# The first modulation of a transformer block: from column sums to rows turned into columns

## The chip, the cores and the metric

The kernel runs as one program on one core of a Trainium2 chip. The metric is the device time of one execution in microseconds; the times of before are the median of three runs. The trace comes from one more, profiled execution.

## The reference

Two transformer blocks run one after the other over 512 tokens of width 1024; this change lies at the very beginning of the first. There the vector c (1024 numbers) is turned into a shift and a scale for every channel, and the normed input is modulated with them before the first projection:

```
c_act = silu(c)
mod   = c_act @ w_ada + b_ada               # w_ada: 1024 x 6144
sh1, sc1, gt1, sh2, sc2, gt2 = split(mod, 6)
h     = rmsnorm(x, g_mix) * (1 + sc1) + sh1
proj  = h @ w_in                            # 1024 x 2560
```

Only sh1 (columns 0 to 1023 of w_ada) and sc1 (columns 1024 to 2047) are wanted at once; they are 8 MB of weights. The other four parts are computed later, beside other work. After `proj` follow an attention with differences of two softmaxes, a pooling, a gated convolution, a gated feed-forward layer, and a second block with three attentions and a large mixture of experts.

## The kernel before

Everything is kept transposed: channels on the 128 partitions, eight chunks of 128 channels (`xT[:, k, :]`, k from 0 to 7), 512 tokens along the free dimension. A product of full precision is made from split operands: each weight block and each chunk of h is cut into a high part (a copy to fp32r on ACT, `wh` in L87, `hh` in L556) and a low part (the difference on VectorE, `wl` in L90, `hl` in L559), and `product` issues three matrix products of 512 columns, high x high (L431), high x low (L432), low x high (L433).

The program's order is written out by hand: each engine executes its instructions in the order in which the code issues them, and waits there for what they need. A `Stream` loads weight blocks of 512 KB on SP's queue into four buffers (`wr`), and splits each when the code asks for it (`stream.until`, `stream.get`).

The opening goes like this. SP's queue loads two modulation blocks, x in eight pieces, more modulation blocks, the first three blocks of `w_in`, and the rest of the modulation blocks; ACT's queue loads c broadcast to all partitions (`cb`) and small vectors, POOL's queue two constants. The modulation is computed in two ways. A block `ada[j]` holds 128 output channels on the partitions and 1024 inputs along the free dimension; VectorE multiplies it by silu(c), held on all partitions (`silc`), and sums along the row into one column of `mod` (`mod_chunk`, L331). This is done for the eight chunks of the shift and, as `ADAP` is 4, for the first four of the scale. The last four chunks of the scale are sums on TensorE (`scale_sums`, L516): a 128 x 128 piece of weights is the stationary side, one column of silu(c) (`silk`) moves, and eight of those add up into one column of `ps_sc`.

Beside this, the squares of x are added up chunk by chunk (L411, L414 on ACT, L415 on VectorE), TensorE sums them over the channels (`token_sums`, L391), VectorE takes the reciprocal root in small steps (`rsqrt`, L369 to L377), and TensorE and ACT spread it over the partitions (L384, L543).

The first three blocks of `w_in` are then multiplied as one group (`gemm2`): for each chunk k, `h_ready(k)` issues the making of `hh[k]`, of the next chunk's scaled input (`full`, L551) and of `hl[k]`, and the modulation of chunk k + 2; then the nine products of chunk k follow. What leaves the group is split again and sent through a bounce buffer in memory (`restack`) to be laid out for the attention.

Of the kernel before, what the change touches and what calls it, by code (L numbers as in the profile page):

```python
# [33 lines left out]
ORDER_IN2 = [0, 4, 8, 1, 5, 9, 2, 6, 10, 3, 7, 11, 16, 12, 17, 13, 32, 22, 23, 14, 27, 24, 25, 15, 41,  # L34
              26, 35, 18, 19, 34, 36, 28, 44, 20, 37, 21, 45, 29]
ADA_FROM = 4
ADAP = 4
NADA = 3
MEMA = 4
NU = 2  # L40
# [198 lines left out]
def tile_kernel(ctx, tc, a, out):  # L239
# [77 lines left out]
    for i in range(7):  # L317
        tag = "e" if i < P["es"] else "wt"
        ada0.append(wk.tile([128, D], F32, name="ada0", tag=tag, bufs=P["es"] if tag == "e" else 7 - P["es"]))
    cb = wraw.tile([128, D], F32, name="wr")  # L320
    nc.scalar.dma_start(cb, bass.AP(tensor=a["c"].tensor, offset=0, ap=[[0, 128], [1, D]]))
    b_ada = load("b_ada", [128, 48], nc.scalar)
    mod = cst.tile([128, 48], F32, name="mod")
    silc = cst.tile([128, D], F32, name="silc")
    vec = {"g_mix": load("g_mix", [128, 8], nc.scalar)}
    silk = load("c_cols", [128, 8], nc.scalar)
    identf = load("identf", [128, 128], nc.scalar)

    def mod_chunk(key, w):
        j = key[1]  # L330
# [4 lines left out]

    stream.made = made

    def load_ada(*js):
        for j in js:
            nc.sync.dma_start(ada0[j], a["ada"][j] if j < 8 + ADAP else a["ada_sc"][j - 8 - ADAP])  # L340
    load_ada(0, 8)
    for k in range(KD):
        nc.sync.dma_start(xT[:, k, :], a["xT"][:, k, :])
    load_ada(12, 1, 9, 13)
    stream.RAW = 3
    stream.load()
    ada0.append(wraw.tile([128, D], F32, name="wr"))
    load_ada(14, 15, 2, 10, 3, 11, 4, 5, 6, 7)
    nc.scalar.activation(silk, silk, AF.Silu)
    nc.scalar.activation(silc, cb, AF.Silu)  # L350
    ones = cst.tile([128, 1], F32, name="ones")
    nc.vector.memset(ones, 1.0)

# [157 lines left out]
    nc.vector.tensor_scalar(b_sc, b_ada[:, 8:16], 1.0, None, op0=OP.add)  # L511
    ps_sc = pst.tile([128, 512], F32, name="pt")

    def scale_sums(k):
        for i in range(KD):
            nc.tensor.matmul(ps_sc[:, k:k + 1], ada0[8 + k][:, 128 * i:128 * i + 128], silk[:, i:i + 1],  # L516
                             start=i == 0, stop=i == KD - 1)

    def modulation(k):
        mod_chunk(("ada", k), ada0[k])  # L520
        if k < ADAP:
            mod_chunk(("ada", 8 + k), ada0[8 + k])
            nc.vector.scalar_tensor_tensor(gs[:, k:k + 1], mod[:, 8 + k:9 + k], 1.0, vec["g_mix"][:, k:k + 1],
                                           op0=OP.add, op1=OP.mult)
            return
        nc.vector.scalar_tensor_tensor(gs[:, k:k + 1], ps_sc[:, k:k + 1], b_sc[:, k:k + 1], vec["g_mix"][:, k:k + 1],
                                       op0=OP.add, op1=OP.mult)

    modulation(0)
    acc = SumSq(S)  # L530
    for k in range(KD):
        tag, n = (("hsq", 2), ("hqs", 2), ("hi", 2), ("lo", 2))[k // 2]
        acc.add(xT[:, k, :], tmp=hn.tile([128, 512], F32, name="sq0", tag=tag, bufs=n))
    stream.ahead = 0
    stream.until(("w_in", ORDER_IN[0]))
    scale_sums(4)
    modulation(1)
    r0 = rsqrt(acc.sums(), [128, 4], 1.0 / D, EPS)
    scale_sums(5)
    stream.until(("w_in", ORDER_IN[2]))  # L540
    Rs = hn.tile([128, S], F32, name="rs0", tag="hqs")
    R = spread(r0, 4)
    nc.scalar.activation(Rs, R, AF.Copy)  # L543
    for k in range(6, KD):
        scale_sums(k)

    hf = {}

# [4 lines left out]

    def h_ready(k):

        nc.scalar.activation(hh[:, k, :], hf[k], AF.Identity, bias=mod[:, k:k + 1])  # L556
        if k + 1 < KD:
            scaled(k + 1)
        nc.vector.scalar_tensor_tensor(hl[:, k, :], hf.pop(k), mod[:, k:k + 1], hh[:, k, :].bitcast(F32),  # L559
                                       op0=OP.add, op1=OP.subtract)  # L560
        if k + 2 < KD:
            modulation(k + 2)


    def head_norm(src, n, g, nh, then, sq=None, qs=None, scaled=False, floor=None):
# [1517 lines left out]
def layout(i):  # L2083
    i = {k: np.asarray(v) for k, v in i.items()}
    r = consts()
    tr = lambda x: np.ascontiguousarray(x[0].T.reshape(KD, 128, -1).transpose(1, 0, 2))
    r["xT"] = tr(i["x"])
    r["mem"] = i["mem_2"].reshape(2, 128, D)
    r["c"] = i["c"].reshape(D)
    r["ada"] = np.ascontiguousarray(i["w_ada"][0].T).reshape(48, 128, D)  # L2090
    r["ada_sc"] = blocks(i["w_ada"][0][:, 128 * (8 + ADAP):2048], 8)
    r["c_cols"] = cols(i["c"])
    r["b_ada"] = cols(i["b_ada"])
    for n, m in (("g_mix", "g_mix"), ("g_ffn", "g_ffn"), ("g_final", "g_final"), ("norm1_g", "norm1_g_2"),
                 ("norm2_g", "norm2_g_2"), ("mem_norm_g", "mem_norm_g_2"), ("g_subln", "g_subln"),
                 ("pool_scale", "pool_scale")):
        r[n] = cols(i[m])
    r["conv_w"] = np.ascontiguousarray(i["conv_w"][0].reshape(3, 2, 128).transpose(2, 1, 0))
    for n in ("lambda_q1", "lambda_k1", "lambda_q2", "lambda_k2"):
        r[n] = i[n].reshape(32)  # L2100
    r["w_in"] = blocks(i["w_in"][0], 8)
    r["w_mem_kv"] = blocks(i["w_mem_kv_2"][0], 8)
    r["w_out"] = blocks(i["w_out"][0], 8)
    r["w_gate_up"] = blocks(i["w_gate_up"][0], 8)
    wd = i["w_down"][0]
    dn = np.zeros((24, 128, 1024), np.float32)
    for g, (f0, f1) in enumerate(FGROUPS):
        dn[8 * g:8 * g + 8, :, :128 * (f1 - f0)] = blocks(wd[128 * f0:128 * f1], f1 - f0)
    r["w_down"] = dn
    wp = np.zeros((128, 2, 128), np.float32)  # L2110
    for g in range(4):
        o = 64 * (g % 2)
        wp[o:o + 64, g // 2, o:o + 64] = i["w_pool"][0, g]
    r["w_pool"] = wp
    w2 = i["w_in_2"][0]
    r["w_in2"] = blocks(np.concatenate([w2[:, :1536], w2[:, 1544:]], axis=1), 8)
    r["w_ff"] = np.ascontiguousarray(w2[:, 1536:1544].reshape(8, 128, 8).transpose(1, 0, 2)).reshape(128, 64)
    r["b_forget"] = i["b_forget_2"].reshape(8, 1)
    r["b_gate"] = cols(i["b_gate_2"])
    hg = [i[n + "_2"][0] for n in ("fox_q_g", "fox_k_g", "swa_q_g", "swa_k_g", "mem_q_g", "mem_k_g")]  # L2120
    r["hg"] = np.ascontiguousarray(np.stack([np.tile(g, 128 // len(g)) for g in hg], axis=1))
    r["sinks"] = i["swa_sinks_2"].reshape(8)
    wo = [i[n][0].reshape(4, 128, 8, 128).transpose(2, 1, 0, 3) for n in ("w_fox_o_2", "w_swa_o_2", "w_mem_o_2")]
    r["w_o01"] = np.ascontiguousarray(np.stack(wo[:2], axis=2)).reshape(8, 128, 1024)
    r["w_o2"] = np.ascontiguousarray(wo[2]).reshape(8, 128, 512)
    r["w_out2"] = blocks(i["w_out_2"][0], 8)
    r["w_pq"] = blocks(i["w_peer_q_2"][0], 8)
    k12 = np.stack([i["peer_keys1_2"][0], i["peer_keys2_2"][0]], axis=1)
    r["keysT"] = np.ascontiguousarray(k12.transpose(0, 1, 3, 2)).reshape(16, 128, 128)
    r["u"] = np.ascontiguousarray(i["peer_u_2"][0].reshape(128, 128, 8, 128).transpose(0, 3, 2, 1)).reshape(128, 128, 1024)  # L2130
    r["v"] = i["peer_v_2"][0].reshape(128, 128, 1024)
    r["u_rows"] = i["peer_u_2"][0]
    r["norm2_row"] = i["norm2_g_2"].reshape(D)
    return r
# [19 lines left out]
```

## Time and profile before

| what | us |
|---|---|
| median of three runs | 2421.26 |
| lowest and highest run | 2417.63 and 2423.24 |
| the profiled execution | 2422.71 |
| its span | 2420.9 |
| PE busy in the span | 2342.7 |
| VectorE busy in the span | 1824.1 |
| ACT busy in the span | 1171.1 |

The span runs from the first to the last instruction that the profile shows; the rest of an execution's time lies around it. Engines are PE (TensorE's products), PEld (its weight loads), DVE (VectorE), ACT (ScalarE), POOL (GpSimd) and SP. Matrix products overlap at their ends, so the distance of two starts, not the length of one, is what a product costs. In a row of the timeline the numbers are the start, the length, the engine, the line and the operation with its tiles, and in brackets the idle time before it and what ended it.

### The profile page before, as it was taken

The page shows a single profiled execution, that of the slowest core. Times are in us where ns is not written, and L with a number is a line of the kernel's source. Part 1 is how long each engine was busy: PE and PEld are TensorE (multiplying, and loading weights), DVE is VectorE, ACT ScalarE, POOL GpSimd, SP SyncE. Part 2 cuts the span into 40 slices and gives each one's busy share as a digit, 9 for nine tenths or more (in the row PEclk, how much of TensorE's full clock was granted, in tenths as well). Part 3 has the DMA queues.
Part 4 walks back from the last instruction along what each step waited for, and adds up shares of the span by engine and source line. Part 5 has one row for each costly group of instructions (what it writes and reads, how often), then busy time and mean ns, then how long its engine had stood idle before and what let it go on. Part 6 is the DMA issues. An engine that isn't in the chain of part 4 may idle for free.

```text
span 2420.9 us, 36478 instructions
## 1 busy us (share of the span) xinstructions
PE 2342.7 (97%) x13131; PEld 2096.7 (87%) x13131; DVE 1824.1 (75%) x3640; ACT 1171.1 (48%) x2168; POOL 581.0 (24%) x566
## 2 busy tenths in 40 slices
PE   5899999999999999999999999999999999999998
PEld 5677788888877888877788899999999999999998
DVE  6678776555577777655588898788886789888886
ACT  3466445344455555443345444567995333333332
POOL 0410101000002210000000233343323456555552
PEclk9999999999999999999999999999999999999999
DMA  7873769888837653223424999999999999999995
GB/s 265 214 204 106 232 210 312 283 292 283 276 110 217 161 138 107 77 78 118 144 81 166 344 376 399 350 382 375 373 346 382 390 379 391 399 397 404 399 387 198
DMA packets 213876, 650.27 MB, mean 269 GB/s; under 512 B 26624, under 2 KB 62208, under 8 KB 213312
## 3 DMA queue, kind: packets, MB, share of 16 engines
q1 hardware_dynamic: 140624, 404.68, 47.1%
q0 software_dynamic: 72352, 242.65, 28.9%
q8 instruction: 103, 1.69, 0.3%
q10 hardware_dynamic: 720, 0.62, 0.1%
q14 instruction: 77, 0.63, 0.1%
HBM read 551.99 MB, written 95.52 MB: 267 GB/s over the span
## 4 chain that ended last, share of the span: by engine, by line
PE 83%; DMA 7%; DVE 5%; issue 2%; ACT 2%; SPq 1%; POOL 1%; ACTq 0%; DVEq 0%; POOLq 0%
PE pg L431 18%; PE pg L433 17%; PE pg L432 17%; PE pv L2017 7%; PE pv L2018 7%; PE pv L2016 7%; DMA ub<-in_u_rows,idx 2%; PE pt L656 1%; DMA wl<-made 1%; PE ps L1821 1%; PE po L678 1%; PE ps L782 1%; PE po L582 1%; DMA ks<-bounce 1%; DMA a_d<-au 1%
## 5 line engine op out<-in xcount | busy, mean ns | idle before, releaser
L431 PE MATMUL pg<-hh,wh 128*128 128x512 f32 (+1 forms) x2088 | 783.7, 375 | 10.2 <-ACT au L1952 2.4
L433 PE MATMUL pg<-hh,wl 128*128 128x512 f32 (+1 forms) x2088 | 758.0, 363 | 10.0 <-DMA wl<-made 8.7
L432 PE MATMUL pg<-hl,wh 128*128 128x512 f32 (+1 forms) x2088 | 756.8, 362 | 1.6 <-DVE hl L559 1.4
L87 ACT ACTIVATE wh<-wr 128x1024 fp32r<-128x1024 f32 (+2 forms) x446 | 465.5, 1044 | 382.4 <-PE pv L2017 213.6
L433 PEld LDWEIGHTS pg<-hh,wl 128*128 128x128 f32 x2088 | 394.2, 189 | 58.5 <-DMA wl<-made 10.9
L431 PEld LDWEIGHTS pg<-hh,wh 128*128 128x128 f32 x2088 | 394.6, 189 | 49.3 <-ACT au L1952 3.0
L432 PEld LDWEIGHTS pg<-hl,wh 128*128 128x128 f32 x2088 | 395.7, 190 | 35.3 <-DVE hl L559 2.6
L219 DVE TENSOR_TENSOR wl<-wr,wh 128x1024 fp32r<-128x1024 f32 x212 | 258.7, 1221 | 22.6 <-ACT wh L87 19.6
L1707 POOL DMA_INDIRECT ub<-in_v,idx x128 | 209.4, 1636 | 185.7 <-DVE rows_o L219 160.6
L90 DVE TENSOR_TENSOR wl<-wr,wh 128x1024 fp32r<-128x1024 f32 (+2 forms) x176 | 209.3, 1191 | 45.7 <-ACT wh L87 43.9
L1707 POOL DMA_INDIRECT ub<-in_u_rows,idx x128 | 164.5, 1285 | 248.0 <-DVE dots L219 216.7
L219 DVE CUSTOM_DVE_ANT_0 ub<-ub,rows_h 128x1024 f32<-128x1024 f32 x128 | 154.8, 1218 | 24.7 <-DMA ub<-in_u_rows,idx 23.4
L2016 PE MATMUL pv<-part,wh 128*128 128x368 f32 x512 | 169.3, 331 | 0.6 <-ACT ag L1949 0.6
L2017 PE MATMUL pv<-parts,wh 128*128 128x368 f32 x512 | 169.8, 332 | 0.0
L2017 PE MATMUL pv<-part,wh 128*128 128x368 f32 x512 | 169.5, 331 | 0.0
L2018 PE MATMUL pv<-parts,wl 128*128 128x368 f32 x512 | 169.3, 331 | 0.0
L2018 PE MATMUL pv<-part,wl 128*128 128x368 f32 x512 | 168.8, 330 | 0.0
L2016 PE MATMUL pv<-parts,wh 128*128 128x368 f32 x512 | 168.0, 328 | 0.0
L219 DVE SCALAR_TENSOR_TENSOR rows_o<-ub,dots,rows_o 128x1024 f32<-128x1024 f32 x127 | 162.7, 1281 | 7.0 <-DMA ub<-in_v,idx 5.8
L1868 ACT ACTIVATE ogh<-oh,gT 128x128 f16<-128x128 f16 x368 | 114.7, 438 | 8.9 <-issue 4.8
L97 DVE TENSOR_TENSOR pl<-wr,ph 128x1024 fp32r<-128x1024 f32 x58 | 70.9, 1222 | 51.9 <-ACT ph L95 51.9
L99 POOL DMA_DIRECT2D made<-pl x58 | 30.8, 532 | 297.4 <-DVE pl L97 297.4
(426 smaller groups left out, 4071.3 us busy)
## 6 DMA issues: line engine op xcount, KB each, us to landing
wr<-in_u SPq DMA_DIRECT2D x186, 512.0 KB
wr<-in_v SPq DMA_DIRECT2D x128, 512.0 KB
wr<-in_w_in SPq DMA_DIRECT2D x66, 512.0 KB
made<-pl POOLq DMA_DIRECT2D x58, 512.0 KB
wl<-made POOLq DMA_DIRECT2D x58, 512.0 KB
g_d<-stg SPq DMA_DIRECT2D x32, 736.0 KB
ag<-g_d SPq DMA_DIRECT2D x32, 736.0 KB
wr<-in_w_gate_up SPq DMA_DIRECT2D x44, 512.0 KB
```

The lines of the kernel that those rows point to most:

```text
L87: self.nc.scalar.activation(hi[:, :n], t[:, :n], AF.Copy)
L90: self.low.tensor_tensor(lo[:, :n], t[:, :n], hi[:, :n].bitcast(F32), op=OP.subtract)
L97: self.low.tensor_tensor(lo, t, hi.bitcast(F32), op=OP.subtract)
L219: return f(*args, **kw)
L431: nc.tensor.matmul(ps[:m, :n], w[0][:, wk], rh, start=first, stop=False)
L432: nc.tensor.matmul(ps[:m, :n], w[0][:, wk], rl, start=False, stop=False)
L433: nc.tensor.matmul(ps[:m, :n], w[1][:, wk], rh, start=False, stop=last)
L1707: nc.gpsimd.indirect_dma_start(out=got[n], out_offset=None, in_=flat["u" if what in "ux" else "v"], in_offset=bass.IndirectOffsetOnAxis(ap ...
L1868: nc.scalar.activation(og[:, 1, n // 2, :, n % 2], oh1[:, n // 2, :, n % 2], AF.Copy, scale=gT[:, tk.start + n:tk.start + n + 1])
L2016: nc.tensor.matmul(ps, wh[:, c], hi, start=i == 0, stop=False)
L2017: nc.tensor.matmul(ps, wh[:, c], lo, start=False, stop=False)
L2018: nc.tensor.matmul(ps, wl[:, c], hi, start=False, stop=i == 127)
```

## The change

The modulation of shift and scale is computed with the other operand stationary. `silk` holds silu(c) as eight columns of 128; a column is loaded as the stationary side, and 512 columns of weights move through it (`ada_r`, a new layout of the same 8 MB: block 4g + i holds inputs 256 i to 256 i + 255 for 512 outputs). Eight such products give a row of 512 outputs on one partition (`mod_row(g)`), ACT copies it out, and four small products with a one turn its four pieces into columns (`mod_cols(g)`), from which VectorE makes `gs` and `mod`. Rows 0 and 2 are the halves of the scale, rows 1 and 3 those of the shift. Rows 0 and 1 are issued before the group of products, rows 2 and 3 within it, at chunks 2 and 4.

The order of the opening changes with it: x is loaded first, in four pieces, then modulation blocks 0 to 7, three blocks of `w_in`, and modulation blocks 8 to 15; c in columns is the first load of ACT's queue and c in rows the last, and `silc`, which later chunks of the modulation still use, is made after the squares. The three `w_in` blocks are split after rows 0 and 1; before, the splits of the first one stood ahead of the reciprocal root.

```diff
--- before.py
+++ after.py
@@ -34,7 +34,6 @@
 ORDER_IN2 = [0, 4, 8, 1, 5, 9, 2, 6, 10, 3, 7, 11, 16, 12, 17, 13, 32, 22, 23, 14, 27, 24, 25, 15, 41,
               26, 35, 18, 19, 34, 36, 28, 44, 20, 37, 21, 45, 29]
 ADA_FROM = 4
-ADAP = 4
 NADA = 3
 MEMA = 4
 NU = 2
@@ -317,14 +316,14 @@
     for i in range(7):
         tag = "e" if i < P["es"] else "wt"
         ada0.append(wk.tile([128, D], F32, name="ada0", tag=tag, bufs=P["es"] if tag == "e" else 7 - P["es"]))
-    cb = wraw.tile([128, D], F32, name="wr")
-    nc.scalar.dma_start(cb, bass.AP(tensor=a["c"].tensor, offset=0, ap=[[0, 128], [1, D]]))
+    silk = load("c_cols", [128, 8], nc.scalar)
     b_ada = load("b_ada", [128, 48], nc.scalar)
     mod = cst.tile([128, 48], F32, name="mod")
     silc = cst.tile([128, D], F32, name="silc")
     vec = {"g_mix": load("g_mix", [128, 8], nc.scalar)}
-    silk = load("c_cols", [128, 8], nc.scalar)
     identf = load("identf", [128, 128], nc.scalar)
+    cb = wraw.tile([128, D], F32, name="wr")
+    nc.scalar.dma_start(cb, bass.AP(tensor=a["c"].tensor, offset=0, ap=[[0, 128], [1, D]]))
 
     def mod_chunk(key, w):
         j = key[1]
@@ -335,19 +334,16 @@
 
     stream.made = made
 
-    def load_ada(*js):
-        for j in js:
-            nc.sync.dma_start(ada0[j], a["ada"][j] if j < 8 + ADAP else a["ada_sc"][j - 8 - ADAP])
-    load_ada(0, 8)
-    for k in range(KD):
-        nc.sync.dma_start(xT[:, k, :], a["xT"][:, k, :])
-    load_ada(12, 1, 9, 13)
+    for k in range(0, KD, 2):
+        nc.sync.dma_start(xT[:, k:k + 2, :], a["xT"][:, k:k + 2, :])
+    for j in range(8):
+        nc.sync.dma_start(ada0[j], a["ada_r"][j])
     stream.RAW = 3
     stream.load()
     ada0.append(wraw.tile([128, D], F32, name="wr"))
-    load_ada(14, 15, 2, 10, 3, 11, 4, 5, 6, 7)
+    for j in range(8, 16):
+        nc.sync.dma_start(ada0[j], a["ada_r"][j])
     nc.scalar.activation(silk, silk, AF.Silu)
-    nc.scalar.activation(silc, cb, AF.Silu)
     ones = cst.tile([128, 1], F32, name="ones")
     nc.vector.memset(ones, 1.0)
 
@@ -511,38 +507,46 @@
     nc.vector.tensor_scalar(b_sc, b_ada[:, 8:16], 1.0, None, op0=OP.add)
     ps_sc = pst.tile([128, 512], F32, name="pt")
 
-    def scale_sums(k):
-        for i in range(KD):
-            nc.tensor.matmul(ps_sc[:, k:k + 1], ada0[8 + k][:, 128 * i:128 * i + 128], silk[:, i:i + 1],
-                             start=i == 0, stop=i == KD - 1)
-
-    def modulation(k):
-        mod_chunk(("ada", k), ada0[k])
-        if k < ADAP:
-            mod_chunk(("ada", 8 + k), ada0[8 + k])
-            nc.vector.scalar_tensor_tensor(gs[:, k:k + 1], mod[:, 8 + k:9 + k], 1.0, vec["g_mix"][:, k:k + 1],
-                                           op0=OP.add, op1=OP.mult)
-            return
-        nc.vector.scalar_tensor_tensor(gs[:, k:k + 1], ps_sc[:, k:k + 1], b_sc[:, k:k + 1], vec["g_mix"][:, k:k + 1],
-                                       op0=OP.add, op1=OP.mult)
-
-    modulation(0)
+    rows0 = []
+
+    def mod_row(g):
+
+        ps = pss.tile([128, 512], F32, name="ps")
+        for k in range(KD):
+            nc.tensor.matmul(ps[0:1, :], silk[:, k:k + 1], ada0[4 * g + k // 2][:, 512 * (k % 2):512 * (k % 2) + 512],
+                             start=k == 0, stop=k == KD - 1)
+        row = hn.tile([128, 512], F32, name="row0", tag="lo" if g % 2 else "hi", bufs=2)
+        nc.scalar.activation(row[0:1, :], ps[0:1, :], AF.Copy)
+        rows0.append(row)
+
+    def mod_cols(g):
+
+        for i in range(4):
+            nc.tensor.matmul(ps_sc[:, 4 * g + i:4 * g + i + 1], rows0[g][0:1, 128 * i:128 * i + 128], ones[0:1, :],
+                             start=True, stop=True)
+        c = slice(4 * (g // 2), 4 * (g // 2) + 4)
+        if g % 2:
+            nc.vector.tensor_tensor(mod[:, c], ps_sc[:, 4 * g:4 * g + 4], b_ada[:, c], op=OP.add)
+        else:
+            nc.vector.tensor_tensor(gs[:, c], ps_sc[:, 4 * g:4 * g + 4], b_sc[:, c], op=OP.add)
+            nc.vector.tensor_tensor(gs[:, c], gs[:, c], vec["g_mix"][:, c], op=OP.mult)
+
     acc = SumSq(S)
     for k in range(KD):
         tag, n = (("hsq", 2), ("hqs", 2), ("hi", 2), ("lo", 2))[k // 2]
         acc.add(xT[:, k, :], tmp=hn.tile([128, 512], F32, name="sq0", tag=tag, bufs=n))
-    stream.ahead = 0
-    stream.until(("w_in", ORDER_IN[0]))
-    scale_sums(4)
-    modulation(1)
-    r0 = rsqrt(acc.sums(), [128, 4], 1.0 / D, EPS)
-    scale_sums(5)
-    stream.until(("w_in", ORDER_IN[2]))
+    nc.scalar.activation(silc, cb, AF.Silu)
+    sums = acc.sums()
+    mod_row(0)
+    r0 = rsqrt(sums, [128, 4], 1.0 / D, EPS)
     Rs = hn.tile([128, S], F32, name="rs0", tag="hqs")
     R = spread(r0, 4)
     nc.scalar.activation(Rs, R, AF.Copy)
-    for k in range(6, KD):
-        scale_sums(k)
+    mod_cols(0)
+    mod_row(1)
+    mod_cols(1)
+    stream.ahead = 0
+    stream.until(("w_in", ORDER_IN[2]))
 
     hf = {}
 
@@ -553,13 +557,18 @@
 
     def h_ready(k):
 
+        if k == 2:
+            mod_row(2)
+        elif k == 3:
+            mod_cols(2)
+        elif k == 4:
+            mod_row(3)
+            mod_cols(3)
         nc.scalar.activation(hh[:, k, :], hf[k], AF.Identity, bias=mod[:, k:k + 1])
         if k + 1 < KD:
             scaled(k + 1)
         nc.vector.scalar_tensor_tensor(hl[:, k, :], hf.pop(k), mod[:, k:k + 1], hh[:, k, :].bitcast(F32),
                                        op0=OP.add, op1=OP.subtract)
-        if k + 2 < KD:
-            modulation(k + 2)
 
 
     def head_norm(src, n, g, nh, then, sq=None, qs=None, scaled=False, floor=None):
@@ -2088,7 +2097,8 @@
     r["mem"] = i["mem_2"].reshape(2, 128, D)
     r["c"] = i["c"].reshape(D)
     r["ada"] = np.ascontiguousarray(i["w_ada"][0].T).reshape(48, 128, D)
-    r["ada_sc"] = blocks(i["w_ada"][0][:, 128 * (8 + ADAP):2048], 8)
+    wa = i["w_ada"][0].reshape(4, 2, 128, -1).transpose(0, 2, 1, 3)
+    r["ada_r"] = np.ascontiguousarray(np.concatenate([wa[..., o:o + 512] for o in (1024, 0, 1536, 512)])).reshape(16, 128, D)
     r["c_cols"] = cols(i["c"])
     r["b_ada"] = cols(i["b_ada"])
     for n, m in (("g_mix", "g_mix"), ("g_ffn", "g_ffn"), ("g_final", "g_final"), ("norm1_g", "norm1_g_2"),
```

## Rows read from the trace of the kernel before

**Rows 1.** Windows: length, busy (instructions) of each engine, clock, DMA share, GB/s.

```profile
37.40:59.90 22.50, 19.48 (x73) 14.43 (x73) 18.08 (x39) 6.59 (x10) 0.53 (x1) 1.00 0.32 101
...
82.00:2420.90 2338.90, 2296.27 (x12937) 2057.89 (x12937) 1779.96 (x3555) 1146.31 (x2133) 568.52 (x544) 0.99 0.76 269
```

**Rows 2.** Timeline of the opening: start, length, engine, line.

```profile
12.39 4.11 ACT L414 ACTIVATE sq<-xT 128x512 f32<-128x512 f32 x7
...
14.60 5.47 DVE L415 TENSOR_TENSOR acc<-acc,sq 128x512 f32<-128x512 f32 x7
...
21.20 1.85 PE L391 MATMUL po<-ones,acc 128*128 128x1 f32 x8
22.82 1.06 ACT L87 ACTIVATE wh<-wr 128x1024 fp32r<-128x1024 f32 x1 [6.32 <-DMA wr<-in_w_in]
...
29.70 2.36 DVE L90 TENSOR_TENSOR wl<-wr,wh 128x1024 fp32r<-128x1024 f32 x2
...
30.99 0.60 ACT L543 ACTIVATE rs<-pt 128x512 f32<-128x512 f32 x1 [4.56 <-PE pt L384]
...
37.43 0.78 PE L431 MATMUL pg<-hh,wh 128*128 128x512 f32 x1
```

**Rows 3.** Line groups within the first group of products, 37.4 to 59.9 us.

```profile
L331 DVE CUSTOM_DVE_ANT_0 ada<-ada,silc,c_b_ada 128x1024 f32<-128x1024 f32 x6 | 7.6, 1279 | 0.0
...
L559 DVE SCALAR_TENSOR_TENSOR hl<-full,mod,hh 128x512 fp32r<-128x512 f32 x7 | 5.2, 748 | 0.3 <-ACT hh L556 0.2
L551 DVE SCALAR_TENSOR_TENSOR full<-xT,gs,rs 128x512 f32<-128x512 f32 x6 | 4.5, 749 | 0.1
L556 ACT ACTIVATE hh<-full,mod 128x512 fp32r<-128x512 f32 x6 | 4.2, 718 | 9.3 <-DVE full L551 9.3
```

**Rows 4.** Timeline of PE within that group: two products early, two later.

```profile
39.28 0.63 PE L432 MATMUL pg<-hl,wh 128*128 128x512 f32 x1
...
39.71 0.63 PE L433 MATMUL pg<-hh,wl 128*128 128x512 f32 x1
...
41.20 0.40 PE L431 MATMUL pg<-hh,wh 128*128 128x512 f32 x1
...
41.43 0.40 PE L432 MATMUL pg<-hl,wh 128*128 128x512 f32 x1
```

**Rows 5.** Timeline at the end of the group and at PE's next long wait.

```profile
59.48 0.39 PE L433 MATMUL ps<-hh,wl 128*128 128x512 f32 x1
...
81.93 0.77 PE L782 MATMUL ps<-ks,qs 128*128 128x512 f32 x1 [9.23 <-DMA ks<-bounce]
```

**Rows 6.** Line group of the opening, 0 to 40 us: busy time, mean ns.

```profile
L516 PE MATMUL pt<-c_c_cols,ada 128*128 128x1 f32 x48 | 10.5, 349 | 17.8 <-DMA ada<-in_ada_sc 17.8
```

**Rows 7.** Timeline of PE around fp32 products with 256 moving columns.

```profile
101.65 1.94 PE L678 MATMUL po<-wt,v 128*64 128x256 f32 x8
103.52 0.50 PE L782 MATMUL ps<-ks,qs 128*128 128x512 f32 x1
```

**Rows 8.** Windows of the opening.

```profile
0.00:5.00 5.00, 0.00 (x0) 0.00 (x0) 0.06 (x1) 1.28 (x1) 1.47 (x6) 1.00 0.61 179
5.00:10.00 5.00, 0.00 (x0) 0.00 (x0) 0.17 (x1) 0.00 (x0) 0.00 (x0) 1.00 1.08 349
10.00:15.00 5.00, 0.00 (x0) 0.00 (x0) 2.97 (x6) 4.19 (x8) 0.00 (x0) 1.00 1.06 367
...
20.00:25.00 5.00, 5.00 (x25) 5.00 (x25) 1.17 (x2) 1.97 (x2) 0.00 (x0) 1.00 1.03 415
```

**Rows 9.** Windows around PE's idle stretch from 72.7 to 81.9 us.

```profile
74.00:76.00 2.00, 0.00 (x0) 0.00 (x0) 0.00 (x0) 0.00 (x0) 1.92 (x3) 0.76 1.21 288
...
84.00:86.00 2.00, 2.00 (x8) 1.58 (x8) 0.17 (x1) 0.17 (x1) 0.00 (x0) 0.68 0.00 0
```

**Rows 10.** Line group, whole span: one-column fp32 products at a later stage.

```profile
L398 PE MATMUL po<-ones,acc 128*128 128x1 f32 x8 | 0.9, 240 | 0.0
```

## Prediction

> **What bounds the kernel now.** I read the windows view first, in stretches set by hand. From 82 us to the end PE is busy for 2296 of 2339 us [rows 1]: there the kernel is a stream of products with almost no gaps, and whatever delays the start of that stream delays the end by as much. So the question is only when the first group of three `w_in` blocks (the `gemm2` of L431 to L433, 72 products) ends; the change touches nothing behind it.
>
> The timeline of the opening [rows 2] shows why the first of those products starts at 37.43. The weights of the modulation and x arrive first, `w_in` only at 22.8 (ACT's first `wh` waited for that DMA); VectorE adds the squares until 20.07; PE makes the token sums at 21.20 and then the scale sums of L516, the last group of which ends where the first product begins. Inside the group VectorE sets the pace: in the 22.5 us of the stretch [rows 1] it is busy 18.1, of which six modulation sums of 1.28 us are 7.6 and the `hl` and `full` steps 5.2 and 4.5 [rows 3]. 72 products at 0.23 us (41.20 to 41.43 [rows 4]) would need 16.6. The last one starts at 59.48 and its record ends at 59.87; the chain then goes through a bounce in memory, and PE's next idle time, 9.23 us before 81.93, waits for that bounce [rows 5].
>
> **What is removed.** The scale sums on PE (64 instructions of one column, 48 of which are 10.5 us [rows 6]) and twelve modulation sums on VectorE, 12 x 1.28 = 15.4 us, six of them in the group.
>
> **What is added: four rows.** Each is eight products of fp32 data, one stationary column, 512 moving ones. No such product is in the trace. The nearest is L678, fp32 with 256 moving columns: four products in the code are eight instructions in the trace, from 101.65 to 103.52, where the next begins, so about 0.225 us for an instruction of 256 columns at the upper clock [rows 7]. A 512-column one should cost twice that, 0.45 us; a product is two, 0.90 us, and a row sixteen, 7.2 us. Bounds: 0.23 us for one instruction if it went like the 512-column fp32r product [rows 4], 3.7 us a row; and 0.90 us at the lower clock, 14.4 us a row. I take 0.45, since L678 is the same data type and its price went with the moving columns, which the change does not reduce. One stationary column saves only weight loading, which already overlaps.
>
> The Trainium skill, page "TensorE: Matmul & The Clock Gate", section "Back-to-back issue gap", gives about 131 ns for a sustained 512-column product; by it 64 instructions would be an estimated 8.4 us instead of 28.8, and the change would cost almost nothing. The trace disagrees for fp32r: 0.23 us in an unbroken run [rows 4].
>
> **The opening, step by step.** DMA: x is 2.1 MB and now first, but c (0.5), `corr` (0.5, POOL's queue) and the small loads share the engines. The DMA moved 0.90 MB by 5 us, 2.64 by 10, 4.48 by 15 [rows 8]: x is in between 8.5 us (2.1 MB) and 11.8 us (3.3 MB); I take 11. Two squares of 0.6 and one sum of 0.7 behind it [rows 2]: 13.1. Token sums 1.85 [rows 2]: 15.1. Row 0 starts there; its four blocks need 5.4 MB, about 17.3 us, and the last is wanted after 20, so these loads are hidden (5 us of margin; without it the delay is theirs).
>
> Row 0 starts at the lower of the two clock levels. The clock column reads 1.00 all through the opening, but 512-column products are 0.43 us apart at 39.28 and 0.23 at 41.20 [rows 4]: 1.2 GHz until about 40.9, 3.5 us after products began. Likewise, work resumed at 81.93 [rows 5] and the slice 84 to 86 has a mean clock of 0.68 [rows 9], so it rose about 85.3: 3.4 us at the lower level. So row 0 has four instructions of 0.90, then twelve of 0.45: 8.9 us, to 24.0. ACT copies the row (0.60 as L543 [rows 2], plus 0.2 to drain): 24.8. The reciprocal root and its spread lie under that. Eight one-column instructions turn it, 0.9 us for eight in L398 [rows 10], taken as 1.0: 25.8. Row 1, 7.2: 33.0; copy 0.8: 33.8. Its columns (1.0) and one small sum: 35.0. Now the code splits the three `w_in` blocks, and this is where the move costs: ACT's `wh` and VectorE's `wl` stand in their engines' queues behind the copy and the sum, though the blocks came at about 26 (9.1 MB). Three `wl` of 1.2 [rows 2]: 38.6. `full` 0.7, `hh` 0.7 [rows 3]: first product at 40.0, 2.6 us later than the 37.43 of before.
>
> SP's next three `w_in` loads and the small constants behind them wait for these splits too and go from 29 to about 36; they are used in the group or after, so I cost that at nothing; if the cover fails, a constant is late by a few us inside the group.
>
> **The group.** From 40.0: 72 products, 16.6. First `hl`, 0.7. PE stood still from 34.8 to 40.0; in the trace it fell to half speed about 75.0 (mean 0.76 in the slice 74 to 76 [rows 9]), 2.3 us after it had stopped at 72.7 (the idle 9.23 us before 81.93 [rows 5]), so it will start slow again: 3.4 us at half speed are 1.7, I take 1.5 as part of them is a wait. Row 2: 7.2. Behind it stands ACT, in order: copy 0.8, `hh` 0.7, then `hl` 0.7, less one product 0.2: 2.0. Columns 1.0. Two small sums 0.4, `full` 0.7, `hl` 0.7, less 0.2: 1.6. Row 3: 7.2, copy 0.8, columns 1.0; sum 0.2, `hh` 0.7, `hl` 0.7, less 0.2: 1.4. Together 41.0, against 22.4 before: +18.6. VectorE's relief is real (1.5 us a step against PE's 2.07), but it is worth only the 5.8 us from 22.4 to 16.6, and the two rows with their turns and waits cost 22.2.
>
> **Sum.** +2.6 +18.6 = +21.2. The profiled execution took 2422.7 (span 2420.9 and 1.8 around it); it becomes 2443.9. It was 1.4 over the median of 2421.26, so I forecast 2442.5.
>
> **Rivals.**
> *The rows stay at the lower clock* (slower still). For it: between 20 and 25 us PE was busy without a gap, with 25 instructions in 5 us [rows 8], and still ran at the lower level (eight one-column sums took 1.85 us there [rows 2], 0.9 later [rows 10]): one-column work did not raise the clock, and here one stationary column is used. Against: the moving side is 512 columns, as in the products that raised it. Price: row 0 +5.5, row 1 +7.2, the two turns +1.6; rows 2 and 3 would lose the clock after some 2.3 us as in the idle stretch (+5.0 each) and hand 3.4 slow us to the products after them (+1.7 each): +27.7, 2470. [...]
> *The rows are cheap* (not slower). If an instruction with one stationary column costs less than its moving columns, the total moves by 64 x (0.45 - p): nothing is lost at p = 0.12 us, and under 0.05 it is a gain above 0.2%, which is about what a measurement here can tell from no change. For it: only that such an instruction is not in the trace. Against: L678. At p = 0.13 it gives 2422. The page's 131 ns would be this case.
> *The delay is swallowed behind the group.* PE idles 9.23 us for the bounce; if that transfer did not wait for the group, +12 would be left, 2433. Against: the bounce is written from the group's own result, so it moves along.
>
> **How the numbers follow.** Forecast 0.73 (its own range 2436 to 2449: x earlier or later by 2, row instruction 0.43 to 0.47, turns and waits by a few us); slow rows, wholly or in part, 0.12; cheap rows 0.09; swallowed 0.06. Leaving out the full slow case and most of the cheap one, the range is 2431 to 2456. Faster by more than 0.2%: 0.04, all from very cheap rows. Within 0.2%: 0.07, cheap rows and a swallowed delay beyond the 9.23. Slower: 0.89.
>
> **What would show it.** Right: the square sums end near 13 us instead of 20; 64 new instructions of 512 columns about 0.45 us apart, the first few 0.9; `wh` of `w_in` waiting on ACT until about 34 with its DMA long in; first L431 near 40; two stretches of about 10 us within the group without its products; last product near 81; everything behind it shifted by the same 21. Wrong: rows under 4 us, rows of 14 us, or a wait for the bounce that shrinks.

## The result, and the profile after

The changed kernel took 2442.96 us as the median of four runs (2442.25 to 2445.68), against 2421.78 for four of the kernel before: the ratio, estimated over all runs (so not exactly the quotient of the medians), is 1.0094, interval 1.0080 to 1.0107. A second, separate series (e11 below) gave 2447.82 for four runs against 2420.3, ratio 1.0115, interval 1.0100 to 1.0129. The change is slower by about 1%; the intervals meet from 1.0100 to 1.0107, which of 2420 us is 24 to 26.

The windows view of the new profile, cut at the start and the end of the first group and at the end of PE's wait for the bounce, answers to [rows 1].

```profile
40.20:84.20 44.00, 38.85 (x120) 20.56 (x120) 12.01 (x26) 8.10 (x13) 0.00 (x0) 0.89 0.12 37
...
107.70:2441.60 2333.90, 2292.77 (x12937) 2053.86 (x12937) 1779.32 (x3555) 1149.17 (x2133) 584.95 (x544) 1.00 0.76 269
```

The group takes 44 us instead of 22.5; VectorE is now busy for 12 of them instead of 18, so it no longer paces it. Behind the bounce PE is busy for 2293 of 2334 us, much as before.

The timeline of the opening in the changed kernel answers to [rows 2].

```profile
11.94 1.15 ACT L410 ACTIVATE sq<-xT 128x512 f32<-128x512 f32 x2 [1.83 <-DMA xT<-in_xT]
12.61 1.49 DVE L411 TENSOR_TENSOR acc<-acc,sq 128x512 f32<-128x512 f32 x2 [1.49 <-ACT sq L410]
...
14.15 1.86 PE L387 MATMUL po<-ones,acc 128*128 128x1 f32 x8 [14.15 <-DVE acc L411]
...
15.94 8.80 PE L516 MATMUL ps<-ada,c_c_cols 128*1 128x512 f32 x16
...
24.78 0.59 ACT L519 ACTIVATE row<-ps 1x512 f32<-1x512 f32 x1 [10.73 <-PE ps L516]
...
25.41 1.05 PE L525 MATMUL pt<-ones,row 1*128 1x1 f32 x8
...
26.39 7.03 PE L516 MATMUL ps<-ada,c_c_cols 128*1 128x512 f32 x16
...
33.95 2.93 ACT L86 ACTIVATE wh<-wr 128x1024 fp32r<-128x1024 f32 x3
...
35.26 3.50 DVE L89 TENSOR_TENSOR wl<-wr,wh 128x1024 fp32r<-128x1024 f32 x3
...
40.23 0.80 PE L427 MATMUL pg<-hh,wh 128*128 128x512 f32 x1 [5.08 <-ACT hh L567]
```

The last squares wait for x until 11.94; the sum is there at 14.1 instead of 20.07. Row 0 is sixteen instructions in 8.80 us, row 1 sixteen in 7.03. Note that ACT's three `wh` begin only at 33.95, behind ACT's copy of row 1, and VectorE's `wl` at 35.26, behind the sum that makes `mod` from the columns of row 1. The first product starts at 40.23, 2.8 us later than before.

The timeline of PE inside the group stands against [rows 4] and [rows 5]; in brackets is the idle time before an instruction and what ended it.

```profile
46.20 7.03 PE L516 MATMUL ps<-ada,c_c_cols 128*1 128x512 f32 x16
54.52 0.50 PE L427 MATMUL pg<-hh,wh 128*128 128x512 f32 x1 [1.29 <-ACT hh L567]
...
57.37 1.05 PE L525 MATMUL pt<-ones,row 1*128 1x1 f32 x8
...
60.32 0.66 PE L428 MATMUL pg<-hl,wh 128*128 128x512 f32 x1 [1.47 <-DVE hl L570]
60.78 0.63 PE L429 MATMUL pg<-hh,wl 128*128 128x512 f32 x1
61.20 0.63 PE L427 MATMUL pg<-hh,wh 128*128 128x512 f32 x1
...
63.90 5.31 PE L516 MATMUL ps<-ada,c_c_cols 128*1 128x512 f32 x12
69.05 1.88 PE L516 MATMUL ps<-wr,c_c_cols 128*1 128x512 f32 x4
71.66 1.05 PE L525 MATMUL pt<-ones,row 1*128 1x1 f32 x8 [0.74 <-ACT row L519]
73.72 0.49 PE L427 MATMUL pg<-hh,wh 128*128 128x512 f32 x1 [1.01 <-ACT hh L567]
...
83.77 0.39 PE L429 MATMUL ps<-hh,wl 128*128 128x512 f32 x1
```

Row 2 runs from 46.20 to 53.2, row 3 from 63.90 to 70.9, and each drags pauses behind it: 1.29 us for `hh`, 1.47 for `hl`, 1.01 for `hh`. From 60.78 to 61.20 products are 0.43 us apart again. The windows view of those places shows the granted clock, as column eight of [rows 9] does (after the five busy times).

```profile
59.00:60.00 1.00, 0.00 (x0) 0.00 (x0) 1.00 (x2) 0.00 (x0) 0.00 (x0) 1.00 0.00 0
60.00:61.00 1.00, 0.68 (x2) 0.59 (x3) 0.67 (x3) 0.00 (x0) 0.00 (x0) 0.75 0.00 0
...
64.00:65.00 1.00, 1.00 (x3) 0.17 (x2) 0.00 (x0) 0.00 (x0) 0.00 (x0) 1.00 0.00 0
...
74.00:75.00 1.00, 0.71 (x2) 0.49 (x2) 1.00 (x6) 0.99 (x2) 0.00 (x0) 0.57 0.00 0
```

It fell at about 60.5 and at 74.1, to 1.2 GHz, and was back up in the slice 64 to 65, after the products of chunk 3. The last product starts at 83.77. The end of the chain in [rows 5] then looks as before.

```profile
83.52 0.33 SPq L655 DMA_DIRECT2D bounce<-hi  x1
...
107.66 0.77 PE L791 MATMUL ps<-ks,qs 128*128 128x512 f32 x1 [9.11 <-DMA ks<-bounce]
```

PE waits 9.11 us for the bounce, against 9.23, and resumes at 107.66 instead of 81.93. The length of that wait varies between executions: a second trace of the kernel before (e5) has 6.48 and resumes at 80.19, a second one of the changed kernel (e11) has 8.09 and resumes at 107.80.

### The profile page after: what moved, and what is told of

Its sections match the earlier page's. It is cut to its first block, busy times and chain, and to the rows that moved or that the text cites. A ratio compares the mean times of both kernels' runs of the same rounds, so it can differ in the third digit from the quotient of the medians.

```text
span 2441.6 us, 36518 instructions
## 1 busy us (share of the span) xinstructions
PE 2364.1 (97%) x13163; PEld 2090.6 (86%) x13163; DVE 1808.9 (74%) x3614; ACT 1175.6 (48%) x2172; POOL 597.5 (24%) x566
## 3 DMA queue, kind: packets, MB, share of 16 engines
q1 hardware_dynamic: 140048, 404.68, 46.4%
## 4 chain that ended last, share of the span: by engine, by line
PE 84%; DMA 5%; DVE 5%; ACT 3%; issue 2%; POOL 1%; DVEq 0%; ACTq 0%; SPq 0%; POOLq 0%
PE pg L427 18%; PE pg L429 17%; PE pg L428 17%; PE pv L2026 7%; PE pv L2027 7%; PE pv L2025 7%; DMA ub<-in_u_rows,idx 2%; PE ps L1830 1%; PE pt L665 1%; PE po L687 1%; DMA ada<-in_ada_r 1%; DMA ks<-bounce 1%; PE ps L791 1%; PE po L591 1%; DVE ub L218 1%
## 5 line engine op out<-in xcount | busy, mean ns | idle before, releaser
L1716 POOL DMA_INDIRECT ub<-in_v,idx x128 | 217.9, 1703 | 178.8 <-DVE rows_o L218 165.0
L1716 POOL DMA_INDIRECT ub<-in_u_rows,idx x128 | 169.7, 1326 | 242.3 <-DVE dots L218 208.8
L218 DVE CUSTOM_DVE_ANT_0 ub<-ub,rows_h 128x1024 f32<-128x1024 f32 x128 | 154.5, 1218 | 22.4 <-DMA ub<-in_u_rows,idx 22.2
L96 DVE TENSOR_TENSOR pl<-wr,ph 128x1024 fp32r<-128x1024 f32 x58 | 70.9, 1223 | 51.9 <-ACT ph L94 51.9
```

The costliest lines, as they stand in the source:

```text
L96: self.low.tensor_tensor(lo, t, hi.bitcast(F32), op=OP.subtract)
L218: return f(*args, **kw)
L1716: nc.gpsimd.indirect_dma_start(out=got[n], out_offset=None, in_=flat["u" if what in "ux" else "v"], in_offset=bass.IndirectOffsetOnAxis(ap ...
```

## The experiments

Times below are medians, ratios are against the kernel before on the same chip. "Bounce" is the start of the first transfer that carries a result of the group to memory, 59.23 in the trace of before and 83.52 after. In these traces it starts 0.64 us before the end of the group's last product, so it marks the end of the group. The line of before:

```profile
59.23 0.33 SPq L646 DMA_DIRECT2D bounce<-hi  x1
```

**e1, the new place of x alone.**

```diff
     def load_ada(*js): ...
-    load_ada(0, 8)
-    for k in range(KD):
-        nc.sync.dma_start(xT[:, k, :], a["xT"][:, k, :])
-    load_ada(12, 1, 9, 13)
+    for k in range(0, KD, 2):
+        nc.sync.dma_start(xT[:, k:k + 2, :], a["xT"][:, k:k + 2, :])
+    load_ada(0, 8, 12, 1, 9, 13)
```

> The kernel before with one part of the change alone: x loaded ahead of the modulation blocks, all else as before. Theory (the four rows on PE are the cost, the order of loads is not): the squares end near 14 us instead of 20, but the reciprocal root still stands behind the split of the first w_in block, whose place in the load order is the same; first product 36 to 38 us, time 2419 to 2425. Rival (the order of the loads is what costs): 2430 or more.

2418.46, ratio 0.9994 (0.9984 to 1.0004); first product at 36.22, bounce at 57.1. First product and bounce came as the theory said, the time 0.5 us below its range; one step did not come. In the timeline of e1 the sums of squares end at 22.1, later than before (20.07), not earlier:

```profile
16.62 5.46 DVE L414 TENSOR_TENSOR acc<-acc,sq 128x512 f32<-128x512 f32 x7
...
22.14 1.87 PE L390 MATMUL po<-ones,acc 128*128 128x1 f32 x8 [2.00 <-DVE acc L414]
```

They stand behind the modulation of chunk 0 in VectorE's queue, whose block now arrives behind x (at 14.01, after 5.33 us of waiting); ACT's squares were late as well, from 13.65, as c in columns was in only at 12.59. The order of the loads neither costs nor brings anything that can be measured.

**e2, a quarter of the columns.** The copy of a row and the pieces that are turned are cut to the same quarter.

```diff
-  matmul(ps[0:1, :], silk[:, k:k + 1], ada0[...][:, 512 * (k % 2):512 * (k % 2) + 512], ...)
+  matmul(ps[0:1, :128], silk[:, k:k + 1], ada0[...][:, 512 * (k % 2):512 * (k % 2) + 128], ...)
```

> The changed kernel with each row product cut to 128 of its 512 moving columns (three quarters of the shift and scale are left out; the first quarter stands in for them): same instructions, loads, copies and order, a quarter of the columns. Theory (a row costs by its moving columns): a row falls from 7.0 us to about 1.8 at the upper clock and 3.7 at the lower; rows 0 and 1 then wait for their loads, first product near 32, the group ends near 65.5, time 2424 (2419 to 2429). Rival (the turns, the waits and the place of the w_in splits cost, not the columns): 2436 or more.

2425.35, ratio 1.0024 (1.0012 to 1.0035), bounce at 62.4. PE in the timeline of e2:

```profile
15.97 3.57 PE L516 MATMUL ps<-ada,c_c_cols 128*1 128x128 f32 x16
...
30.03 0.79 PE L427 MATMUL pg<-hh,wh 128*128 128x512 f32 x1 [5.31 <-ACT hh L567]
...
36.33 1.91 PE L516 MATMUL ps<-ada,c_c_cols 128*1 128x128 f32 x16
...
42.06 1.05 PE L525 MATMUL pt<-ones,row 1*128 1x1 f32 x8
...
45.01 0.50 PE L428 MATMUL pg<-hl,wh 128*128 128x512 f32 x1 [1.47 <-DVE hl L570]
45.35 0.40 PE L429 MATMUL pg<-hh,wl 128*128 128x512 f32 x1
45.58 0.39 PE L427 MATMUL pg<-hh,wh 128*128 128x512 f32 x1
```

Row 0 takes 3.57 us and row 2 1.91, as forecast; the first product came 2 us earlier than forecast and the group ended 2.4 earlier. With the same instructions, loads and turns, and copies that are 0.3 us shorter each, about 21 us of the bounce's delay are gone (83.5 to 62.4); the four rows together are 20.6 us shorter. The last lines matter further down: behind the same turn and the same 1.47 us of waiting as at 57 to 60 in the changed kernel, products here are 0.23 us apart. A row costs by its moving columns, and that is most of the change's price.

**e3, the splits ahead of row 1.**

```diff
     mod_cols(0)
+    stream.ahead = 0
+    stream.until(("w_in", ORDER_IN[2]))
     mod_row(1)
     mod_cols(1)
-    stream.ahead = 0
-    stream.until(("w_in", ORDER_IN[2]))
```

> The changed kernel with the three w_in blocks split before row 1 instead of behind its columns. Theory: the splits go under row 1; first product 37.0 instead of 40.2, and PE's pause before it becomes about 2 us, so the clock stays up: 3 to 5 us less, 2438 to 2440. Rival (the place of the splits is the main cost): 10 us less or more, under 2433. Rival (it is hidden): 2443.

2444.48 (four runs), ratio 1.0108 (1.0086 to 1.0129). The timeline of e3's opening is as forecast:

```profile
26.24 2.94 ACT L86 ACTIVATE wh<-wr 128x1024 fp32r<-128x1024 f32 x3
...
26.78 7.03 PE L516 MATMUL ps<-ada,c_c_cols 128*1 128x512 f32 x16
...
27.32 3.50 DVE L89 TENSOR_TENSOR wl<-wr,wh 128x1024 fp32r<-128x1024 f32 x3
...
37.20 0.56 PE L427 MATMUL pg<-hh,wh 128*128 128x512 f32 x1 [1.67 <-ACT hh L567]
```

The splits lie under row 1 and the first product starts at 37.20. One step did not come: PE waited for only 0.68 and 1.67 us beside the turn of row 1, but the group's products are 0.43 us apart until 40.7 all the same, so the clock did not stay up. The bounce came at 80.85, 2.7 us earlier than after. The time, forecast at 2438 to 2440, does not show it; its interval is wider than the gain. The placement is a small term, seen in the trace alone.

**e4, all rows ahead of the group.**

```diff
     stream.until(("w_in", ORDER_IN[2]))
+    for g in (2, 3):
+        mod_row(g)
+        mod_cols(g)
...
-        if k == 2:
-            mod_row(2)
-        elif k == 3:
-            mod_cols(2)
-        elif k == 4:
-            mod_row(3)
-            mod_cols(3)
```

> The changed kernel with rows 2 and 3 and their columns issued before the group instead of at chunks 2 and 4, the splits left where they are. Same work on every engine. Theory: what the group loses beside the rows themselves is the waits of PE around them and the two falls of the clock; with the rows in one run the first product is near 54.5 and the group ends near 72 instead of 84.2, time 2431 (2427 to 2435). Rival (the rows are merely paid for wherever they stand): group end within 2 us of 84, time 2441 to 2445.

2437.96 (four runs), ratio 1.0085 (1.0060 to 1.0109), bounce at 73.16, 10.4 us earlier than after. PE in the timeline of e4:

```profile
35.03 7.03 PE L516 MATMUL ps<-ada,c_c_cols 128*1 128x512 f32 x16
...
54.12 0.80 PE L427 MATMUL pg<-hh,wh 128*128 128x512 f32 x1 [1.67 <-ACT hh L563]
```

The same rows and turns in one run, first product at 54.12 (forecast 54.5). By this trace about 10 of the change's 24 us are not the rows' work but where rows 2 and 3 stand: the pauses around them, the splits that nothing covers, and the clock; how the 10 divide was not tried, and e4 still has its first thirteen products at the lower level (0.43 us apart until 60.2). The time missed the forecast of 2427 to 2435: it is 17.6 us above before, where the two series of the changed kernel have 21.2 and 27.5, and the interval overlaps theirs, so the 10 us rest on the trace.

**e5, the kernel before again; e6, the rows added to it; e11, the changed kernel again.** In the first pair of traces the bounce moved by 24.3 us but the end of the span by 20.7. Is a later start paid back in part?

> The kernel before itself, profiled once more, to see how much the stretches behind the group move from one execution to the next. In the first two traces the group's end moved by 24.3 us and the end of the program by 20.7; PE's waits for the low parts kept in memory were 8.7 us before and 6.4 after. Theory (the 3.6 us between are chance): the opening repeats within 0.5 us, the later stretches differ by 2 to 4 us, time 2418 to 2424. Rival (a later start is paid back in part): the second trace of before has the same 8.7 us and the same span within 1 us.

> The kernel before with 32 of the new row products added ahead of the group, their result unused, nothing taken out. Theory (64 instructions of 0.43 us, the first four at the lower clock, on the path): 29 us on PE; the first product at 67, the group PE-bound behind it (VectorE runs ahead in the meantime) and done at 83.5, 24 later than before; time 2443 (2440 to 2447). Rival (a later start is paid back in part): the same opening, but 2436 to 2440.

```diff
     for k in range(6, KD):
         scale_sums(k)
+    ps = pss.tile([128, 512], F32, name="ps")
+    for k in range(32):
+        nc.tensor.matmul(ps[0:1, :], silk[:, k % 8:k % 8 + 1], ada0[14 + k % 2][:, 0:512], start=k == 0, stop=k == 31)
```

> The changed kernel once more, with more runs. Ten traces so far have the end of the program 2349 to 2356 us behind the group's first bounce, whether that bounce came at 57 or at 84. Theory (a later start carries through, the 3.6 us less in the first trace of after were chance): bounce at 83.5 within 0.5, time 24 over before, 2443 to 2446. Rival (a part is paid back): 20 to 21 over before.

e5: 2420.2, ratio 0.9998 (0.9985 to 1.0011). PE's waits for the low parts kept in memory were 8.1 us against 8.7 in the first trace, and its span 2419.8 against 2420.9: taken alone, that looked like the rival. But these waits do not go with the start of the group: they are 6.0 us in e1 and 5.0 in e7, which start earlier, and 6.4 and 5.9 in the two traces of the changed kernel. e6: 2448.57, ratio 1.0127 (1.0108 to 1.0145), 28.9 us more and above the forecast's 2447. e11: 27.5 more, bounce at 84.70, both above the forecast (24 more, 83.5 within 0.5). PE in the timeline of e6:

```profile
66.09 1.02 PE L548 MATMUL ps<-wr,c_c_cols 128*1 128x512 f32 x2
67.05 0.50 PE L431 MATMUL pg<-hh,wh 128*128 128x512 f32 x1
...
83.27 0.39 PE L433 MATMUL ps<-hh,wl 128*128 128x512 f32 x1
```

The 64 instructions end at 67.0 and the group, now paced by PE, follows in 16.6 us; both as forecast to half a microsecond. With nothing taken out, the rows alone move the bounce by 24.3 us against e5. What came behind the bounce in all traces (start of the store of the result less start of the bounce, us):

| trace | bounce | to the end | trace | bounce | to the end |
|---|---|---|---|---|---|
| before | 59.23 | 2353.7 | after | 83.52 | 2350.3 |
| e1 | 57.10 | 2355.9 | e3 | 80.85 | 2351.9 |
| e5 | 58.71 | 2353.1 | e6 | 83.02 | 2350.8 |
| e7 | 58.50 | 2349.1 | e11 | 84.70 | 2351.7 |
| e8 | 57.48 | 2354.1 | e12 | 83.20 | 2350.1 |
| e9 | 54.00 | 2350.9 | e4 | 73.16 | 2355.4 |
| e2 | 62.42 | 2354.3 | e10 | 63.53 | 2354.5 |

The stretch behind the bounce varies by 7 us, with early starts at both ends of it (e7 and e1). The five traces with a bounce behind 80 average 1.8 us less than the six with one before 60, and 2.5 less than all nine others; so few traces with such a spread do not tell this safely from chance. The timed series of e6 and e11 are longer than the bounce's delay, not shorter. That a start 24 us later is paid back is not shown, and the two series speak against a payback of 4 us; one of about 2 us stays possible.

**e7 and e8, can the opening be shortened?** Both load x first and split early. e7 keeps one row (first half of the scale), ten chunks on VectorE and two as one-column sums; e8 has no row, twelve chunks on VectorE and four as one-column sums, as before. The core of e7 (`row_copy` is the copy that stood in `mod_row`):

```diff
-    mod_row(0)
+    ps0 = mod_row(0)
     r0 = rsqrt(sums, [128, 4], 1.0 / D, EPS)
+    shift(0)
+    shift(1)
+    stream.ahead = 0
+    stream.until(("w_in", ORDER_IN[2]))
+    row_copy(ps0)
...
-    mod_cols(0)
-    mod_row(1)
-    mod_cols(1)
+    shift(2)
+    mod_cols(0)
```

> A version that keeps what was good on either side: x first and the splits early; of the modulation one row only (first half of the scale) on PE while it would wait, ten chunks on VectorE (the shift and two of the scale), two chunks as one-column sums in the group. Theory: first product near 28.5, VectorE sets the pace to about 49, the group ends near 51.5 against 59.9 before: 8 us less, 2412 (2408 to 2416). Rival (the rest of the kernel, not the opening, sets the end): 2419 to 2423.

> The kernel before with its split of the modulation (twelve chunks on VectorE, four as one-column sums) but the opening in another order: x first, the reciprocal root and chunk 0 ahead of the splits, one-column sums spread over the group. No rows. Theory: first product near 28 to 30, VectorE-bound to about 51, group end near 52: 7 to 8 us less, 2413 (2409 to 2417). Rival (x first gains nothing without the row): 2419 to 2423, as e1.

e7: 2419.38, ratio 0.9998 (0.9989 to 1.0007), first product at 29.37, bounce at 58.5. e8: 2420.56, ratio 1.0009 (0.9994 to 1.0023), first product at 26.12, bounce at 57.5. The group began 8 to 11 us earlier and ended nearly where it did. The timeline of e7 names what took the gain:

```profile
42.93 0.17 DVE L762 TENSOR_SCALAR c_g_subln<-c_g_subln 128x4 f32<-128x4 f32 x1 [1.11 <-DMA c_g_subln<-in_g_subln]
...
43.55 0.42 ACT L422 ACTIVATE wph<-c_w_pool 128x256 fp32r<-128x256 f32 x1 [6.89 <-DMA c_w_pool<-in_w_pool]
...
49.47 0.19 DVE L766 CUSTOM_DVE_ANT_0 lamv<-lamv 128x32 f32<-128x32 f32 x1 [1.44 <-DMA lamv<-in_lambda_k]
```

Small constants, loaded on SP's queue behind the modulation blocks, are wanted by instructions that stand between the group's own in VectorE's and ACT's queues. The times are those of the rivals, not the 2412 and 2413 of the theories.

**e9 and e10, those constants on POOL's queue.**

```diff
-            nc.sync.dma_start(t, a[n])
+            (nc.sync if n == "rcnt" else nc.gpsimd).dma_start(t, a[n])
...
-            nc.sync.dma_start(lamv[:, i, :], ...)
+            nc.gpsimd.dma_start(lamv[:, i, :], ...)
```

> e7 with the small constants (all but the 512 KB one) loaded on POOL's idle queue instead of behind the modulation blocks on SP's. In e7 VectorE and ACT waited for them inside the group (1.1, 0.7 and 1.4 us on VectorE, 6.9 on ACT), which took the place of the gain. Theory: these waits go, the group ends near 52 instead of 59, time 2413 (2409 to 2416). Rival (another load or wait is next): group end 56 or later, time 2417 to 2421.

> e8 with the small constants on POOL's queue: no rows. Theory (the row adds little beside order and constants): group end 52 to 54, time 2414 (2410 to 2418). Rival (without the row VectorE is too slow): group end 56 or later, 2417 to 2421.

e9: 2416.94, ratio 0.9989 (0.9979 to 0.9999), bounce at 54.0, 5.2 us earlier than before. VectorE and ACT no longer wait for a constant in the group. It beats both kernels, the one before by 3 us, at the edge of what can be measured here; that it beats e7 is shown by the bounce alone, as the intervals of the ratios overlap. The forecast of 2413 was too good, and the group ended 2 to 3 us later than forecast. e10: 2425.32, ratio 1.0015 (1.0004 to 1.0026), bounce at 63.5, outside both theory and rival. In its trace the group ends 6 us later than in e8, which had the same work; the times do not tell the two apart, and the execution that was profiled (2428.49) is among the slower of twelve, from 2417.59 to 2429.41. PE in its timeline shows what happened there:

```profile
47.32 0.63 PE L430 MATMUL ps<-hl,wh 128*128 128x512 f32 x1
47.75 0.63 PE L431 MATMUL ps<-hh,wl 128*128 128x512 f32 x1
48.18 3.41 PE L514 MATMUL pt<-c_c_cols,wr 128*128 128x1 f32 x16
51.45 0.77 PE L429 MATMUL pg<-hh,wh 128*128 128x512 f32 x1
```

Products are 0.43 us apart from 30 until 56, and sixteen one-column sums take 3.41 us where e8 has 1.84: by this spacing the clock stayed at its lower level through 26 us in which PE was nearly always busy. (The clock column of the windows view reads 1.00 there, as it does in the opening of before, where the spacing says 1.2 GHz too.) Runs of nine products of 512 columns alternate there with the one-column sums. VectorE waited up to 5.02 us for these sums, so the group was not late because VectorE was too slow, as the rival had it. In e8, with the same order of work, products were at 0.23 us from 35 on.

**e12, a filler for the pauses.**

```diff
+    def filler():
+        nc.tensor.matmul(ps_sc[0:1, 128:512], silk[:, 0:1], ada0[0][:, 128:512], start=True, stop=True)
...
             mod_row(2)
+            filler()
         elif k == 3:
             mod_cols(2)
+            filler()
         elif k == 4:
             mod_row(3)
             mod_cols(3)
+            filler()
```

> The changed kernel with one product of 384 columns, its result unused, put into each of three pauses of PE in the group: behind row 2, behind the columns of row 2 and behind those of row 3. Theory (the clock falls there because PE had nothing wide to do for about 2.5 us): no fall at 60 or 75, products 0.23 us apart in chunks 3 and 4, the bounce 3 us earlier, 80.5. Rival (the clock falls for another reason): products at 0.43 us again, the bounce at 83.5 or later.

2442.9 in its one run, bounce at 83.2. PE in its timeline, around the second and the third filler:

```profile
59.99 0.81 PE L535 MATMUL pt<-ada,c_c_cols 128*1 128x384 f32 x2 [0.25 <-DVE gs L531]
...
62.21 0.39 PE L427 MATMUL pg<-hh,wh 128*128 128x512 f32 x1
62.44 0.40 PE L428 MATMUL pg<-hl,wh 128*128 128x512 f32 x1
...
75.30 0.63 PE L427 MATMUL pg<-hh,wh 128*128 128x512 f32 x1
75.72 0.63 PE L428 MATMUL pg<-hl,wh 128*128 128x512 f32 x1
```

Behind the second filler the products are 0.23 us apart where the changed kernel had 0.43: that fall is not there. Behind the third they are at 0.43 all the same. The bounce, forecast at 80.5, came nearer to the rival's 83.5. From the start of row 2 to the bounce it is 35.7 us instead of 37.3; the 1.5 us that the first two chunks had lost before that (the clock rose at 46.4, against 43.4) have nothing to do with the filler. That the filler held the clock at 60 is not shown: e2 has the same turn and the same wait at 42 to 45 without a filler, and no fall there either, while e11 and e3 have the fall as the changed kernel does. Why the clock fell in these places stays open.

## Why the prediction was right

**The opening: right, term by term.** Token sums at 14.15 (forecast 13.1, x came about 1 us later), row 0 8.80 (8.9), row 1 7.03 (7.2), the copy 0.59, the turn 1.05 (1.0), first product 40.23 (40.0). The instruction of 512 columns, the price that no row of before showed, is 0.43 us against 0.45 taken from L678; e2 and e6 confirm that it goes by columns and lies on the path in full.

**The clock.** Row 0 took 8.80 us where row 1 took 7.03; the excess is that of about four instructions at the lower level, as forecast. So the clock rose within row 0, every instruction of which has one stationary column, and the rival of slow rows falls. The prediction was also right that PE would begin the group slowly: its first products are 0.43 us apart, as in [rows 4].

**The group: the step that was mis-sized.** The prediction had 41.0 us; from 40.23 to the end of the last product's record at 84.16 it took 43.9. The rows came out 0.2 cheaper each. What was missing are the two falls of the clock inside the group, at 60.5 and 74.1: chunk 3 took 5.4 us and chunk 4 4.1, where 3.7 and 2.6 had been counted (nine products and the wait for `hl`). The pauses themselves were in the sum; two further falls of the clock were not. Both falls stand in the second trace of the changed kernel as well (e11, at 61.8 and 75.4; the group took 44.4 us). The term put at nothing, a constant that comes late in the group, was nothing: no product and no step of VectorE or ACT within the group waited for a load.

**The end.** The sum was +21.2 and the first median moved by +21.2, but that is partly luck: the group ended 24.3 later, and the two executions that were profiled differ by 3.6 in the stretches behind. By the second series and the bounces of the two traces of either kernel (58.71 and 59.23, 83.52 and 84.70) the delay of the group, 24 to 26 us, is the better figure. So the sum was some 3 to 5 us short, which the first median hides.

**The rivals.** Cheap rows: no, an instruction is 0.43 us, and by e2 its columns are what it costs. (The gain of 0.2% would have needed 0.04 us an instruction, not 0.05: 64 x 0.40 less 21.2 is 4.4 us, 0.18%.) Swallowed behind the group: no. The length of PE's wait for the bounce says little, as it varies from 9.23 to 6.48 us between two traces of one kernel; but its end, where PE resumes, moved by 25.7 us from the first trace of before to the first of after, and by 27.6 between the second ones. The Trainium skill's 131 ns for a 512-column product (page "TensorE: Matmul & The Clock Gate", section "Back-to-back issue gap") did not show here either: fp32r products stay 0.23 us apart, and fp32 instructions of 512 columns 0.43.

**What the price is made of.** e4 takes 10 us of the bounce's 24 by moving rows 2 and 3 out of the group; covering the splits alone takes 2.7 (e3). These do not add up with e2's 21, which shortens the rows where they stand. What moving does not take away is that PE took over what VectorE had done beside it: four rows are 30 us of PE's time in place of some 14 us of one-column sums, and in this stretch only 6 us could be won by freeing VectorE.

## What to carry to other kernels

Price a product by its moving columns and its data type, not by how few stationary columns it has: fp32 here went through PE in two instructions of 0.43 us for 512 columns with one stationary column, and 0.225 for 256 with 64 [rows 7], where one fp32r instruction of 512 takes 0.23. Work that another engine does beside the critical one is not free to move; first count what the relieved engine was costing (here 22.4 less 16.6 us). A long instruction run placed inside a paced group costs its own time and again what stands behind it in every in-order queue, the small copies and the clock among them.

## What was not expected of the hardware

The clock fell after two stretches of about 2.9 us (57.4 to 60.3, 70.9 to 73.7) in which PE turned a row for 1.05 us and otherwise paused, with one product of 512 columns in the first of them; the same two falls stand in e3 and e11. But in e2 the first of these stretches stands unchanged (42.1 to 45.0) and products stay 0.23 us apart behind it. And in e10 it did not rise for 26 us of nearly unbroken work, 3.8 us of 512-column products in turn with 3.4 us of one-column sums, while in e8 with the same order of work it rose before 35 (both by the spacing, as the clock column reads 1.00 there). Why the same work gave both, in either case, was not tried.
